# Moving the accumulating transfers of the mixer's weight sums from the attention to the v projection in a hybrid decoder block

## The chip, the cores and the metric

The kernel runs on one core of a Trainium2 chip. The metric is the device time of one execution in microseconds (us); the figure for a kernel is the median of its runs. An engine is named as in the profile: PE is TensorE (PEld its weight loads), DVE is VectorE, ACT is ScalarE, POOL is GpSimd, SP is SyncE, which here only issues transfers. `SPq` and `POOLq` are the instructions of those engines that issue or wait.

## The reference

One decoder block on 1024 tokens of width 1024, all in float32. Two branches read one normalised input: a state-space branch (`y_ssm`) and an attention with a forget gate. They are gated, added and multiplied by `w_mix_out`; then come a cross-attention, a gated feed-forward block and a last norm.

```python
u = rms_norm(h, norm_mix[l])
proj = u @ w_in[l]
u_ssm, q, k, v, f_logit, gate_logits = jnp.split(proj, [SPLIT_Q, SPLIT_K, SPLIT_V, SPLIT_F, SPLIT_G], axis=-1)
...
out_a = glu_a * jax.nn.sigmoid(glu_b)
att = forgetting_attention(q, k, v, f_logit + b_forget[l])
out_b = att @ w_fox_o[l]
gate_a, gate_b = jnp.split(jax.nn.sigmoid(gate_logits), 2, axis=-1)
h = h + (gate_a * out_a + gate_b * out_b) @ w_mix_out[l]
h = h + memory_cross_attention(...)
f_a, f_b = jnp.split(rms_norm(h, norm_ffn[l]) @ w_ffn_in[l], 2, axis=-1)
h = h + (jax.nn.silu(f_a) * f_b) @ w_ffn_out[l]
```

The forgetting attention has 8 heads of 64 and adds to each score the difference of running sums of `log_sigmoid(f_logit)`.

## The kernel before, in words

Every float32 operand is split into a high and a low part (`split`, lines 181 to 185: a cast on ACT into the high part, a subtraction on DVE or POOL into the low part), and a product is three matmuls (`mm3`, lines 172 to 175).

The program is written in stages: the input with its norms, the state-space stage with the gate products (its last instructions write `y_d` and `gate_d`), then `Fox.run`, and the tail from the mixer to the end. In `Fox.run` come, in the text, `prepare_v` (weights of v), eight `values_of_v` (the second half of v and the forget logits), `log_forget` (logarithms of the forget gates on DVE; it needs the small load `bfb`, line 1724), `setup` (constants on POOL, lines 1774 to 1784), four copies of `w_glu` in HBM into another order (`wg_d`, line 1990, 1 MB each), the projections of q and k for the first heads, `cumulate` (running sums, written to HBM as `cum_d`, lines 1762 and 1767), `gate_rows` (reads `cum_d` back into the rows 64 to 67 of the q and k tiles, lines 1840 and 1841), `row_max` for the first head (matmuls of line 1862, which read those rows), and then the loop over the 8 heads.

In that loop each head has 12 units (`scores`): scores on PE (lines 1892, 1893), the exponential on ACT (`pf`, line 1899), and the split of the result into `ph` and `pl`. For 4 of the 12 units the low part `pl` is made on POOL (line 1902), for the others on DVE. PE then multiplies `ph` (lines 1917, 1918) and `pl` (line 1924) with v. Between the units PE also gets the row maxima of the next head and the projection of the head after that.

A scheduler arranges the instructions of each engine ahead of time by its own estimates, keeping data dependences; so the place of an instruction on its engine is not that of its line in the text. `B.behind(ins)` only keeps what is issued in it behind `ins` where both are on the same engine. On the chip each engine then runs its list in order, and a transfer that must wait holds everything behind it on the engine that issues it.

The change is about `mix_sums` (lines 583 to 603). The mixer's product is computed with 7 instead of 8 block products, for which sums of blocks of `w_mix_out` are needed. They are made in HBM (`mt_d`), without any engine's arithmetic: a plain 1 MB copy issued by SP (`put`, line 590) writes one block, and two accumulating transfers of 512 KB issued by POOL (`add`, line 594) add another to it. The six steps depend on each other:

```python
steps = [lambda: (put(5, blk[0, 0]), put(7, blk[0, 1])), lambda: (add(5, 0, 1), add(7, 1, 1)),
         lambda: put(6, dst[5]), lambda: add(6, 1, 1), lambda: put(4, dst[6]), lambda: add(4, 1, 0)]
```

`put(6)` copies what `add(5)` finished, `add(6)` adds to that, `put(4)` copies its result, `add(4)` adds to it: on SP two of the four copies wait for POOL's transfers, and on POOL four of the eight wait for SP's copies. In the kernel before, step h - 1 is issued in the loop of head h, behind `self.spread[h - 1]` (a transfer of SP, line 1939), for h from 1 to 6. The results are read from line 754 on, in the tail.

Of the kernel before, what the change touches and what calls it, by code (L numbers as in the profile page):

```python
# [14 lines left out]
ALU = mybir.AluOpType  # L15
# [4 lines left out]
P = 128  # L20
# [4 lines left out]
NH = 8  # L25
# [9 lines left out]
NEG = -1.0e30  # L35
# [31 lines left out]
def f32(ap):  # L67
    return ap.bitcast(F32)
# [26 lines left out]
def weave(main, side, lead=0):  # L95

    n, m, done = len(main) - lead, len(side), 0
    for i, f in enumerate(main):
        f()
        want = m if i + 1 == len(main) else max(0, (i + 1 - lead) * m // max(n, 1))  # L100
        while done < want:
            side[done]()
            done += 1
# [1573 lines left out]
class Fox:  # L1677
# [69 lines left out]
    def cumulate(self):  # L1747

        B, fp, xl = self.B, self.fp, self.logf
        V, A, G, T, S = B.V, B.A, B.G, B.T, B.S  # L1750
        cum = fp.tile([NH, L], F32, tag="num", name="cum")
        ones8 = self.sh.half("ones8")[0:NH]
        G.memset(ones8, 1.0)
        for b in range(2):
            ps = B.bank(("misc", "pv")[b])
            for t in range(4):
                T.transpose(ps[0:NH, t * P:(t + 1) * P], xl[:, (4 * b + t) * NH:(4 * b + t + 1) * NH], B.ident)
            V.tensor_tensor_scan(out=cum[:, 512 * b:512 * b + 512], data0=ones8, data1=ps[0:NH, :],
                                 initial=0.0 if b == 0 else cum[:, 511:512], op0=ALU.mult, op1=ALU.add)
        cch = fp.tile([NH, L], F32R, tag="rb", bufs=2, name="cch")  # L1760
        A.copy(cch, cum)
        S.dma_start(self.cum_d[:, 0, :], f32(cch))
        for b in range(2):
            cs = slice(512 * b, 512 * b + 512)
            cl = fp.tile([NH, 512], F32R, tag="pl", bufs=4, name="cl")
            V.tensor_sub(cl, cum[:, cs], f32(cch[:, cs]))
            S.dma_start(self.cum_d[:, 1, cs], f32(cl))

    def setup(self):
        fp, G = self.fp, self.B.G  # L1770
        self.hb = [[self.sh.tmp("hb", F32R) if i == 0 else fp.tile([P, L], F32R, name=f"hb{s}") for s in range(4)]
                   for i in range(2)]
        for K1, K2, Q1, Q2 in self.hb:
            G.memset(f32(K1[64:69, :]), 1.0)
            G.memset(f32(Q1[64:69, :]), -1.0)

        self.tri = fp.tile([P, 512], F32, name="tri")
        G.memset(self.tri, 0.0)
        G.affine_select(out=self.tri[:, 384:512], in_=self.tri[:, 384:512], pattern=[[-1, P]], compare_op=ALU.is_ge,
                        fill=NEG, base=0, channel_multiplier=1)  # L1780
        self.trk = fp.tile([P, P], F32, name="trk")
        G.memset(self.trk, 0.0)
        G.affine_select(out=self.trk, in_=self.trk, pattern=[[1, P]], compare_op=ALU.is_ge, fill=NEG, base=0,
                        channel_multiplier=-1)
        self.maxed = self.scored = None
        self.pj, self.mc, self.pvs, self.num, self.rb, self.raw = {}, {}, {}, {}, {}, {}
        self.hi_todo, self.lo_todo, self.spread, self.maxima = [], [], {}, {}
# [170 lines left out]
    def run(self, y_d, yT, aT, w_glu, w_d, filler, sums):  # L1958
        B, fp, S = self.B, self.fp, self.B.S
        self.aT = aT  # L1960
        self.prepare_v()
        for t in range(NT):
            self.values_of_v(1, t)
        self.log_forget()
        self.setup()

        def load_y(k, h):

            with B.behind(self.maxima[NH - 2] if h else self.spread[NH - 4]):
                for i, dst in enumerate(yT.rhs(k, h)):  # L1970
                    S.dma_start(f32(dst).rearrange("p (t c) -> p t c", t=4),
                                y_d[k, i, 4 * h:4 * h + 4].rearrange("t p c -> p t c"))

        def first_glu(i, f):
            with B.behind(self.spread[3] if i < 9 else self.maxima[NH - 2]):
                f()

        def load_att(k):
            for h in range(2):
                for i, dst in enumerate(aT.rhs(k, h)):  # L1980
                    S.dma_start(f32(dst), self.att_d[i, k * P:(k + 1) * P, 512 * h:512 * h + 512])

        pro = [self.project(h) for h in range(NH)]
        for h in range(2):
            loaded = pro[h].load()
            pro[h].split()

        with B.tc.issue_after(loaded.ins):
            for k in range(4):
                S.dma_start(w_d[k].rearrange("(m g) c -> m g c", g=8),  # L1990
                            w_glu[k * P:(k + 1) * P].rearrange("(g m) c -> m g c", m=16))
        for f in pro[0].parts[:8] + pro[0].evac[:1] + pro[0].parts[8:] + pro[0].evac[1:]:
            f()
        self.values_of_v(0, 0)
        self.cumulate()
        for t in range(1, 4):
            self.values_of_v(0, t)
        for h in range(2):
            self.gate_rows(h)
        for f in pro[1].parts[:4]:  # L2000
            f()
        weave(pro[1].parts[4:8] + pro[1].evac[:1] + pro[1].parts[8:], self.row_max(0))
        pro[2].load()
        turned = self.max_row(0)
        with B.behind(self.negated):
            ready = pro[1].evac[1](pro[2].split)
        self.values_of_v(0, 4)
        pro[3].load()
        self.values_of_v(0, 5, ready)
        with B.behind(turned):  # L2010
            self.values_of_v(0, 6, ready)
        units = [(qc, kt) for qc in range(2) for kt in range(4 * qc + 4)]
        for h in range(NH):
            side = {i: [] for i in range(12)}
            late = h == NH - 2
            if late:
                for i, f in enumerate(pro[h + 1].parts[8:]):
                    side[i // 2].append(f)
                side[3].append(pro[h + 1].evac[1])
            if h + 1 < NH:  # L2020
                for i, f in enumerate(self.row_max(h + 1)):
                    side[(RSLOT_LATE if late else RSLOT)[i]].append(f)
                side[9].append(lambda: self.max_row(h + 1))
            if h + 2 < NH:
                n = 8 if h + 3 == NH else 16
                for i, f in enumerate(pro[h + 2].parts[:n]):
                    side[i if n == 8 else PSLOT[i]].append(f)
                side[9].append(pro[h + 2].evac[0])
                if n == 16:
                    side[11].append(pro[h + 2].evac[1])  # L2030
            if h + 3 < NH:
                side[9].append(lambda: pro[h + 3].split(self.exp))
            for n_ in {1: (4, 5), 2: (6,), 3: (7,)}.get(h, ()):
                side[5].append(lambda n_=n_: pro[n_].load(self.spread[h - 1]))
            if h == 0:
                side[0].append(lambda: self.values_of_v(0, 7))
            elif h < 7:
                side[5].append(lambda: sums[h - 1](self.spread[h - 1]))
            if late:
                for k in range(8):  # L2040
                    side[4 + k].append(lambda k=k: load_y(k % 4, k // 4))
            if h == NH - 1:
                for k in range(3):
                    side[6 + k].append(lambda k=k: load_att(k))
                for i, f in enumerate(filler):
                    side[i * 12 // len(filler)].append(lambda i=i, f=f: first_glu(i, f))
            for i, u in enumerate(units):
                self.scores(h, *u)
                for f in side[i]:
                    f()  # L2050
                if len(self.hi_todo) > 2:
                    self.values_hi()
                if len(self.lo_todo) > 1:
                    self.values_lo()
                if h and i == 5:
                    with B.behind(self.left):
                        self.divide(h - 1)
        while self.hi_todo:
            self.values_hi()
        while self.lo_todo:  # L2060
            self.values_lo()
        self.divide(NH - 1)
# [29 lines left out]
```

## Time and profile before

| | |
|---|---|
| median of 3 runs | 1574.99 us (1570.75 to 1575.76) |
| profiled execution | 1571.02 us |
| its span, first to last instruction | 1569.0 us |
| mean granted PE clock | 0.986 |
| busy: PE, DVE, ACT, POOL | 97%, 66%, 43%, 17% of the span |

The profile is of one execution. Its own time stands 2 us above its span and 4 us below the median of the runs. A timeline row gives the start in us from the span's start, the duration in us, the engine, the line, the operation, the tiles written and read, and in brackets the idle time of the engine before it and what ended that time. A row of the waits gives the total in us, the number of waits and the longest. A row of the windows gives a stretch, then for PE, PEld, DVE, ACT and POOL the busy us and the number of instructions, then the granted PE clock (1.00 is full), the mean busy share of the 16 DMA engines, and the GB/s that they moved. In the page, PEclk is the clock in tenths over 40 equal slices of 39.2 us.

### The profile page before, as it was taken

The page shows a single profiled execution, that of the slowest core. Times are in us where ns is not written, and L with a number is a line of the kernel's source. Part 1 is how long each engine was busy: PE and PEld are TensorE (multiplying, and loading weights), DVE is VectorE, ACT ScalarE, POOL GpSimd, SP SyncE. Part 2 cuts the span into 40 slices and gives each one's busy share as a digit, 9 for nine tenths or more (in the row PEclk, how much of TensorE's full clock was granted, in tenths as well). Part 3 has the DMA queues.
Part 4 walks back from the last instruction along what each step waited for, and adds up shares of the span by engine and source line. Part 5 has one row for each costly group of instructions (what it writes and reads, how often), then busy time and mean ns, then how long its engine had stood idle before and what let it go on. Part 6 is the DMA issues. An engine that isn't in the chain of part 4 may idle for free.

```text
span 1569.0 us, 20397 instructions
## 1 busy us (share of the span) xinstructions
PE 1521.0 (97%) x7281; PEld 1255.0 (80%) x7281; DVE 1039.4 (66%) x1860; ACT 668.2 (43%) x1187; POOL 268.6 (17%) x349
## 2 busy tenths in 40 slices
PE   8999999999967989999999999999999999999998
PEld 7888888998745768888888888888888888888886
DVE  7936454346645966969965687766677776575555
ACT  6423433325634744223645564333333333354343
POOL 1166641101121213320001200000000000101001
PEclk9999999999978999999999999999999999999999
DMA  9635556620544575856701156555544543797652
GB/s 284 157 104 102 129 136 131 193 24 8 116 75 88 133 205 144 273 174 235 241 29 53 55 212 196 164 162 162 163 155 156 160 147 128 275 393 234 198 161 107
DMA packets 201061, 245.59 MB, mean 157 GB/s; under 512 B 35736, under 2 KB 127816, under 8 KB 200448
## 3 DMA queue, kind: packets, MB, share of 16 engines
q1 hardware_dynamic: 191296, 222.27, 47.6%
q10 hardware_dynamic: 7488, 17.83, 3.0%
q0 software_dynamic: 2176, 4.19, 1.7%
q8 instruction: 57, 0.93, 0.2%
q14 instruction: 44, 0.36, 0.1%
HBM read 173.47 MB, written 81.10 MB: 162 GB/s over the span
## 4 chain that ended last, share of the span: by engine, by line
PE 87%; DVE 4%; DMA 3%; issue 2%; ACT 2%; POOL 1%; SPq 0%; POOLq 0%; DVEq 0%; ACTq 0%
PE mm L1064 15%; PE pv L1064 8%; PE mm L174 7%; PE mm L173 7%; PE mm L175 7%; PE mm L1207 5%; PE sc L1064 4%; PE sc L1207 4%; PE sc L173 3%; PE sc L175 3%; PE sc L174 3%; PE pv L1207 3%; PE mm L772 2%; DMA mt_d<-mt_d 2%; PE misc L1207 2%
## 5 line engine op out<-in xcount | busy, mean ns | idle before, releaser
L184 DVE TENSOR_TENSOR wlo<-raw,whi 128x1024 fp32r<-128x1024 f32 (+2 forms) x122 | 131.3, 1082 | 38.0 <-ACT whi L183 36.9
L183 ACT CAST whi<-raw 128x1024 fp32r<-128x1024 f32 (+2 forms) x122 | 110.8, 912 | 105.8 <-PE mm L174 38.2
L184 DVE TENSOR_TENSOR ol<-or,oh 128x1024 fp32r<-128x1024 f32 x73 | 90.3, 1240 | 73.8 <-ACT oh L183 72.8
L173 PE MATMUL mm<-uh,whi 128*128 128x512 f32 x344 | 138.0, 401 | 0.0
L174 PE MATMUL mm<-ul,whi 128*128 128x512 f32 x344 | 136.5, 397 | 0.0
L175 PE MATMUL mm<-uh,wlo 128*128 128x512 f32 x344 | 135.9, 395 | 0.0
L183 ACT CAST oh<-or 128x1024 fp32r<-128x1024 f32 x73 | 76.8, 1054 | 104.6 <-PE mm L1207 34.2
L1097 POOL TENSOR_TENSOR g<-a,c 128x512 f32<-128x512 f32 x22 | 35.7, 1622 | 389.3 <-ACT a L1096 389.3
L175 PEld LDWEIGHTS mm<-uh,wlo 128*128 128x128 f32 x344 | 65.6, 191 | 13.7 <-DVE wlo L184 0.2
L1899 ACT ACTIVATE pf<-sc 128x512 f32<-128x512 f32 (+1 forms) x96 | 46.5, 489 | 69.2 <-DVE sc L1895 36.6
L1902 POOL TENSOR_TENSOR pl<-pf,ph 128x512 fp32r<-128x512 f32 (+1 forms) x32 | 40.0, 1251 | 207.5 <-DVE ph L1901 201.7
L173 PEld LDWEIGHTS mm<-uh,whi 128*128 128x128 f32 x344 | 65.8, 191 | 11.9
L174 PEld LDWEIGHTS mm<-ul,whi 128*128 128x128 f32 x344 | 65.9, 192 | 11.3
L211 POOL TENSOR_TENSOR r<-ms,mhalf 128x1 f32<-128x1 f32 (+1 forms) x26 | 16.6, 645 | 294.2 <-DVE ms L207 252.8
L1086 DVE SCALAR_TENSOR_TENSOR c<-c,pv 128x512 f32<-128x512 f32 x22 | 15.1, 687 | 77.5 <-ACT c L1085 77.4
L1924 PE MATMUL pv<-pl,vhi 128*65 128x512 f32 (+1 forms) x96 | 33.8, 356 | 29.7 <-POOL pl L1902 29.3
L1064 PE MATMUL pv<-S3h,we 128*128 128x512 f32 x176 | 57.8, 389 | 0.0
L1905 DVE TENSOR_TENSOR pl<-pf,ph 128x512 fp32r<-128x512 f32 (+2 forms) x64 | 35.8, 564 | 20.4 <-ACT ph L1904 19.6
L1924 PEld LDWEIGHTS pv<-pl,vhi 128*65 128x65 f32 x96 | 13.5, 142 | 35.6 <-POOL pl L1902 30.6
L1351 POOL TENSOR_TENSOR sg<-sg,ga 128x512 f32<-128x512 f32 x16 | 29.3, 1852 | 74.0 <-DMA ga<-gate_d 38.6
L1207 PE MATMUL mm<-ol,oh 128*128 128x512 f32 (+1 forms) x110 | 41.9, 381 | 0.0
L1207 PE MATMUL mm<-oh,ol 128*128 128x512 f32 (+1 forms) x110 | 41.9, 381 | 0.0
(661 smaller groups left out, 4635.2 us busy)
## 6 DMA issues: line engine op xcount, KB each, us to landing
or<-c_d SPq DMA_DIRECT2D x77, 256.0 KB
wo<-in_w_ffn_out_dram SPq DMA_DIRECT2D x22, 512.0 KB
c_d<-g SPq DMA_DIRECT2D x44, 256.0 KB
t_d<-wo SPq DMA_DIRECT2D x44, 256.0 KB
or<-t_d SPq DMA_DIRECT2D x44, 256.0 KB
rawb<-in_w_ffn_in_dram SPq DMA_DIRECT2D x20, 512.0 KB
raw<-in_w_ffn_in_dram SPq DMA_DIRECT2D x20, 512.0 KB
raw<-in_w_in_dram SPq DMA_DIRECT2D x19, 512.0 KB
```

The costliest lines, as they stand in the source:

```text
L173: T.matmul(ps, lh, rh, start=first, stop=False)
L174: T.matmul(ps, lh, rl, start=False, stop=False)
L175: return T.matmul(ps, ll, rh, start=False, stop=last)
L183: cast = self.A.copy(hi, src)
L184: self.rest = (self.G if pool_lo else self.V).tensor_sub(lo, src, f32(hi))
L1064: T.matmul(ps, l_[:, k, :], r_, start=first and k == 0 and i == 0, stop=k == 3 and i == 2, skip_group_check=True)
L1097: G.tensor_mul(g[:, 512:], a1, c1)
L1207: T.matmul(ps, l_[:, gi], r_[:, c0:c1], start=k == 0 and (p == NP - LAST if own else p == 0 and n in (1, 2, 7)), stop=p == NP - 1 and k == ...
L1899: self.exp = A.activation(pf[:, off:], ps[:, off:], AF.Exp)
L1902: G.tensor_sub(pl[:, off:], pf[:, off:], f32(ph[:, off:]))
L1905: self.left = V.tensor_sub(pl[:, off:], pf[:, off:], f32(ph[:, off:]))
L1924: self.B.T.matmul(ps[0:65, off:], self.vh[kt // 2][:, kt % 2, h, :], pl[:, off:], start=False, stop=last)
```

## The change

`setup` is called ahead of the eight `values_of_v`, and right behind it all six steps of the sums, with `B.behind` on the last instruction of `setup` (the selection that finishes `trk`, on POOL). They are no longer issued in the loop over the heads. The constant `ones8` moves from `cumulate` into `setup`.

```diff
-        ones8 = self.sh.half("ones8")[0:NH]
-        G.memset(ones8, 1.0)
+        ones8 = self.ones8
...
+        self.ones8 = self.sh.half("ones8")[0:NH]
+        G.memset(self.ones8, 1.0)
         self.tri = fp.tile([P, 512], F32, name="tri")
...
-        G.affine_select(out=self.trk, in_=self.trk, pattern=[[1, P]], compare_op=ALU.is_ge, fill=NEG, base=0,
-                        channel_multiplier=-1)
+        self.ready = G.affine_select(out=self.trk, in_=self.trk, pattern=[[1, P]], compare_op=ALU.is_ge, fill=NEG,
+                                     base=0, channel_multiplier=-1)
...
         self.prepare_v()
+        self.setup()
+        for f in sums:
+            f(self.ready)
         for t in range(NT):
             self.values_of_v(1, t)
         self.log_forget()
-        self.setup()
...
-            elif h < 7:
-                side[5].append(lambda: sums[h - 1](self.spread[h - 1]))
```

On POOL, this is what stands before, from the last constant into the attention's fourth head (`pl` rows are the low parts, four to a head; `mt_d` rows are the accumulating transfers):

```order
L1783 AFFINE_SELECT trk<-trk 128x128
L1753 MEMSET ones_3398 8x512
L1902 TENSOR_TENSOR pl<-pf,ph 128x256
L1902 TENSOR_TENSOR pl<-pf,ph 128x512 x3
L1902 TENSOR_TENSOR pl<-pf,ph 128x256
L1902 TENSOR_TENSOR pl<-pf,ph 128x512 x3
L594 DMA mt_d<-in_w_mix_out_dram 128x2x512 x4
L1902 TENSOR_TENSOR pl<-pf,ph 128x256
L1902 TENSOR_TENSOR pl<-pf,ph 128x512 x3
L1902 TENSOR_TENSOR pl<-pf,ph 128x256
L1902 TENSOR_TENSOR pl<-pf,ph 128x512 x2
L594 DMA mt_d<-in_w_mix_out_dram 128x2x512
```

And this is POOL in the changed kernel, from the same constant:

```order
L1784 AFFINE_SELECT trk<-trk 128x128
L594 DMA mt_d<-in_w_mix_out_dram 128x2x512 x8
L1903 TENSOR_TENSOR pl<-pf,ph 128x256
L1903 TENSOR_TENSOR pl<-pf,ph 128x512 x3
L1903 TENSOR_TENSOR pl<-pf,ph 128x256
```

All eight transfers now stand in one row between the constants and the first `pl` of the first head.

On SP, this is what stands before, from the last stores of the state-space branch (`y_d`) to the read of the running sums:

```order
L1671 DMA y_d<-yh 128x1024
L1671 DMA y_d<-yl 128x1024
L1990 DMA wg_d<-in_w_glu_dram 128x1x2048
L1724 DMA bfb<-in_b_forget_dram 128x8
L1990 DMA wg_d<-in_w_glu_dram 128x1x2048 x3
L1762 DMA cum_d<-cch 8x1024
L1767 DMA cum_d<-cl 8x512 x2
L1800 DMA raw<-in_w_in_dram 128x8x64
L1801 DMA raw<-in_w_in_dram 128x8x64
L1840 DMA hb<-cum_d 2x1024
```

And in the changed kernel (the two rows `mt_d<-mt_d` are `put(6)` and `put(4)`):

```order
L1671 DMA y_d<-yh 128x1024
L1671 DMA y_d<-yl 128x1024
L1993 DMA wg_d<-in_w_glu_dram 128x1x2048
L590 DMA mt_d<-mt_d 128x4x512
L1724 DMA bfb<-in_b_forget_dram 128x8
L1993 DMA wg_d<-in_w_glu_dram 128x1x2048
L590 DMA mt_d<-mt_d 128x4x512
L1993 DMA wg_d<-in_w_glu_dram 128x1x2048 x2
L1761 DMA cum_d<-cch 8x1024
L1766 DMA cum_d<-cl 8x512 x2
L1801 DMA raw<-in_w_in_dram 128x8x64
L1802 DMA raw<-in_w_in_dram 128x8x64
```

Both dependent copies now stand ahead of the running sums, one of them ahead of `bfb` too; the other two copies, `put(5)` and `put(7)`, stand much earlier, here in the changed kernel among the first loads of the gate weights:

```order
L504 DMA kv_d<-kv 128x1024 x2
L158 DMA raw<-in_w_in_dram 128x4x256 x3
L590 DMA mt_d<-in_w_mix_out_dram 128x4x512
L158 DMA raw<-in_w_in_dram 128x4x256
L590 DMA mt_d<-in_w_mix_out_dram 128x4x512
L516 DMA u_d<-us 128x1024
```

They wait for nothing of the v projection, since `B.behind` on a POOL instruction holds only what POOL issues. PE's list is the same up to the attention, and inside the attention it differs by a few exchanges of neighbours.

## The prediction

> **What bounds the kernel now.** I read the page first, then PE's waits in the attention, then POOL's timeline there. PE is busy 97% of the span, so only places where PE stands still or runs slowly can give anything. The clock row of the page has one hole:
>
> ```profile
> span 1569.0 us, 20397 instructions
> PEclk9999999999978999999999999999999999999999
> ```
>
> The two low slices, the 12th and 13th, are those from 431 to 510 us, inside the attention. PE's waits from 397 to 586 us have one large row, and PE's timeline shows its three events:
>
> ```profile
> PE pv L1924 <- POOL pl L1902: 29.3, 3, 14.4
> 450.01 0.47 PE L1924 MATMUL pv<-pl,vhi 128*65 128x256 f32 x1 [14.37 <-POOL pl L1902]
> 500.19 0.69 PE L1924 MATMUL pv<-pl,vhi 128*65 128x512 f32 x1 [10.14 <-POOL pl L1902]
> 553.50 0.69 PE L1924 MATMUL pv<-pl,vhi 128*65 128x512 f32 x1 [4.80 <-POOL pl L1902]
> ```
>
> Each time PE needs a low part that POOL has not made. POOL's timeline says why:
>
> ```profile
> 424.44 1.36 POOL L594 DMA_DIRECT2D mt_d<-in_w_mix_out_dram  x1 [7.91 <-DMA mt_d<-in_w_mix_out_dram]
> 431.36 1.19 POOL L594 DMA_DIRECT2D mt_d<-in_w_mix_out_dram  x1 [5.57 <-issue]
> 438.10 1.15 POOL L594 DMA_DIRECT2D mt_d<-in_w_mix_out_dram  x1 [5.55 <-DMA rb<-rd_d]
> 448.05 1.16 POOL L594 DMA_DIRECT2D mt_d<-in_w_mix_out_dram  x1 [8.80 <-issue]
> 497.68 1.16 POOL L594 DMA_DIRECT2D mt_d<-in_w_mix_out_dram  x1 [15.91 <-DMA mt_d<-mt_d]
> 498.44 1.70 POOL L1902 TENSOR_TENSOR pl<-pf,ph 128x512 fp32r<-128x512 f32 x1
> 503.72 1.17 POOL L594 DMA_DIRECT2D mt_d<-in_w_mix_out_dram  x1 [3.59 <-issue]
> 543.22 1.16 POOL L594 DMA_DIRECT2D mt_d<-in_w_mix_out_dram  x1 [0.41 <-DMA mt_d<-mt_d]
> 551.00 1.15 POOL L594 DMA_DIRECT2D mt_d<-in_w_mix_out_dram  x1 [6.62 <-issue]
> DMA to landing us min/median/max: 5.7/6.6/9.6
> ```
>
> POOL does nothing else at those times: it waits for SP's copy, and between two accumulating transfers it stands as long as the first one takes to land (6.92, 6.74, 9.95, 6.04 and 7.78 us from one to the next, against landings of 5.7 to 9.6). The low part behind them is late by that much.
>
> **What is removed.** To price it with all that follows a stall, I cut the attention at each head's first exponential (line 1899), from head 1 (first row) to head 6 (second row), and took the windows between:
>
> ```profile
> 397.82 0.60 ACT L1899 ACTIVATE pf<-sc 128x512 f32<-128x512 f32 x1
> 560.14 0.60 ACT L1899 ACTIVATE pf<-sc 128x512 f32<-128x512 f32 x1 [5.75 <-DVE sc L1895]
> 397.82:427.60 29.78, 28.73 (x138) 21.53 (x136) 20.27 (x50) 17.84 (x34) 6.93 (x5) 1.00 0.58 136
> 427.60:469.28 41.68, 26.46 (x108) 20.06 (x109) 20.31 (x51) 16.09 (x32) 8.11 (x7) 0.71 0.50 82
> 469.28:506.93 37.65, 27.51 (x124) 20.58 (x123) 20.14 (x51) 16.74 (x33) 6.95 (x6) 0.86 0.43 80
> 506.93:532.81 25.88, 25.83 (x127) 19.20 (x126) 23.48 (x54) 19.71 (x37) 4.59 (x4) 1.00 0.47 110
> 532.81:560.14 27.33, 22.08 (x96) 16.16 (x96) 18.00 (x51) 13.02 (x27) 6.92 (x6) 0.88 0.85 211
> 560.14:585.02 24.88, 23.39 (x111) 16.49 (x111) 20.46 (x46) 14.67 (x28) 4.60 (x4) 1.00 0.67 178
> 420.62 5.83 DMA hb<-mr
> ```
>
> Head 4 (from 506.93) has no accumulating transfer on POOL: 25.88 us, with PE busy 25.83 of it at full clock. That is the price of a head with nothing in its way, and PE is then the bound, DVE (23.48) close behind. Heads 2 and 3 have the same work and take 15.8 and 11.8 us more. Head 1 takes 3.9 us more: the chain of waits has a 4 KB transfer of the row maxima (`hb<-mr`, last row) that took 5.83 us, issued right behind the two 1 MB copies of the sums. Head 5 has half the projection work of head 4, like head 6, which takes 24.88; so its clean time is between 25.88 x 96/127 = 19.6 (by the count of matmuls) and 24.9, the gain 2.4 to 7.7, and I take 5.0, near PE's own wait of 4.80. The sum is 3.9 + 15.8 + 11.8 + 5.0 = 36.5 us. Its bounds are 29.3 (the stalls alone, if the slow clock and the late maxima came from something else) and 39.2 (7.7 for head 5). Nothing else in the attention waits for the sums, and the tail reads them only after it.
>
> **What is moved, on POOL.** The chain of eight now starts when the constants are done and must end by the first `pl`:
>
> ```profile
> 292.17 0.29 POOL L1783 TENSOR_SCALAR_AFFINE_SELECT trk<-trk 128x128 f32<-128x128 f32 x1
> 375.22 0.74 POOL L1902 TENSOR_TENSOR pl<-pf,ph 128x256 fp32r<-128x256 f32 x1 [82.30 <-DVE ph L1901]
> ```
>
> POOL is idle for these 82 us, which covers the chain: eight intervals of 6.92 are 55 us, and the two copies on which it waits took 20.65 and 6.92 us in the attention, the first behind other loads:
>
> ```profile
> 476.63 20.65 DMA mt_d<-mt_d
> 535.89 6.92 DMA mt_d<-mt_d
> ```
>
> With 6.92 for all of them: `add(5)` starts at 292.5 and 299.4 and lands at 306.0; `add(7)` starts at 306.3 and 313.2; `put(6)` leaves SP at 306.1 and lands at 313.0, so `add(6)` follows without a gap at 320.1 and 327.0 and lands at 333.6; `put(4)` leaves at 333.7 and lands at 340.6; `add(4)` ends near 355. That is 20 us before the first `pl`, so POOL costs nothing; without this cover each us late is a us for the first head.
>
> **What is moved, on SP.** Here is the cost. SP's transfers before, the read of the forget bias on DVE, PE's first row maximum with the pass of its wait, and two windows of the DMA engines:
>
> ```profile
> 291.83 0.78 SPq L1990 DMA_DIRECT2D wg_d<-in_w_glu_dram  x1
> 292.71 1.12 SPq L1724 DMA_DIRECT2D bfb<-in_b_forget_dram  x1
> 293.88 7.09 SPq L1990 DMA_DIRECT2D wg_d<-in_w_glu_dram  x3
> 339.76 0.30 SPq L1762 DMA_DIRECT2D cum_d<-cch  x1
> 342.65 0.26 SPq L1840 DMA_DIRECT2D hb<-cum_d  x1
> 323.97 0.22 DVE L1728 TENSOR_TENSOR logf<-fl,bfb 128x64 f32<-128x64 f32 x1
> 351.73 0.22 PE L1862 MATMUL pv<-hb 68*128 68x128 f32 x1
> L1862 PEldq EVENT_SEMAPHORE x1: 51/51/51, 349.6 to 349.6; - x1
> 292.00:309.00 17.00, 17.00 (x119) 15.95 (x118) 3.85 (x8) 4.31 (x7) 0.92 (x3) 1.00 0.95 328
> 343.00:350.00 7.00, 7.00 (x44) 6.28 (x44) 0.42 (x1) 0.37 (x1) 0.00 (x0) 1.00 0.86 98
> ```
>
> `put(6)` now holds SP from 292.7 to 306.1; `bfb` stands behind it and lands with it near 314, 10 us before DVE reads it: hidden. `put(4)` holds SP until 333.7, and two `wg_d` copies stand behind it. In the window from 292 us such copies ran at 328 GB/s, so 1.05 MB takes 3.2 us. If transfers of one queue come out in order, the queue is empty at 340.6 + 6.4 = 347.0. `cum_d`, ready at 339.8 as before, lands near 348, where before `hb<-cum_d` could be issued at 342.65 because it had landed: 5.4 us later. The projection loads (0.5 MB, at 98 GB/s 5.3 us) stand between, as before. PE's wait was passed at 349.6 and its matmul ran at 351.73, so 2.1 us are to spare. PE stands for 5.4 - 2.1 = 3.3 us at its first row maximum; its list goes on in order, so everything after is later by as much. PE also runs slowly behind a stall: head 5, with one of 4.80 us, has a mean clock of 0.88, so 0.12 x 27.33 = 3.3 us of full-clock work is gone, a part of it in the stall itself; I add 2.5 us: 5.8. With the mean interval of 7.49 instead of 6.92 the chain is 3.4 us longer and the cost 9. I take 7. The bounds: 0 with the shortest interval (6.04: `put(4)` 5 us earlier, all covered), and 16 if three of the five intervals ahead of `put(4)` take 9.95, as one beside other traffic did.
>
> The Trainium skill's page "DMA: Bandwidth & Descriptors" (Queues, rings and completion order) says that a DMA engine takes turns between the queues that have work for it, packet by packet; `add(7)` runs beside `put(6)` and a `wg_d` copy, so by that rule it is among the slow ones, and the cost goes towards 16 and the time to 1554.5. In the trace the interval of 9.95 us against 6.04 speaks for the rule, but the window of each is too mixed to show it.
>
> `put(5)` and `put(7)` go among the first loads of gate weights. At 328 GB/s they take 6.4 us; the only load between them is a gate weight too, and the last split of those on ACT waited for PE and not for its load:
>
> ```profile
> 91.52 1.05 ACT L183 CAST whi<-raw 128x1024 fp32r<-128x1024 f32 x1 [3.86 <-PE mm L174]
> ```
>
> So they are free; were they not covered they would cost at most their 6.4 us. `ones8` is a 0.5 us memset on an idle POOL, either way.
>
> The sum is -36.5 + 7 = -29.5 us. The profiled execution took 1571.0 us (span 1569.0), so it would become 1541.5. The runs shown have a median of 1575.0, 4 above it, and I carry the difference over: 1545.5 us.
>
> **The rivals.**
>
> *The accumulating transfers are quick and the copies hide altogether.* With all intervals at 6.04 or below, `put(4)` leaves before 329 and `cum_d` finds an empty queue. The cost is 0 and the time 1575 - 36.5 = 1538.5. For it: SP issued nothing from 301 to 339.8 us before, so there is room, and 5.7 us is the shortest landing. Against it: only one of five intervals was that short, and wg_d copies come in between. The same page of the Trainium skill (Anatomy of one DMA) fits 2.0 us plus bytes over 436e3, an estimate of 3.2 us for 512 KB, and by it this rival would be the answer; the trace's 5.7 to 9.6 for these transfers disagree and decide.
>
> *Slower: SP's head of line becomes the bound.* If the intervals are 9.95, `add(5)` lands at 312; if `put(6)` takes 20.65 it lands at 333, and `add(6)` then at 353; `put(4)` with 20.65 more lands at 374, the two `wg_d` copies at 381, `hb` near 390. PE then stands 38 us at the first row maximum and 2.5 more at a slow clock: 40.5 against 36.5, so 1579. It decides when `put(4)` leaves later than about 360. For it: SP runs in order, and both prices are in the trace. Against it: the 20.65 us copy stood behind projection loads that are not there now.
>
> *The stalls go but not all that I put down to them.* Only the 29.3 us of PE's own waits come back, because the slow clock and the late maxima have other causes (`hb<-mr` still stands behind the projection loads, PE's order has changed a little): 1575 - 29.3 + 7 = 1552.7. For it: DVE is at 23.48 of 25.88 us in the clean head. Against it: that clean head is in the trace.
>
> That the change doesn't do what it says is ruled out by the order of POOL's list, where no transfer stands among the `pl` any more.
>
> **How the numbers follow.** Forecast 0.55, quick transfers 0.17, smaller gain 0.16, SP as the bound 0.12. A measurement of this kernel can tell about 0.3%, 4.7 us, from no change. All of the first three are faster by more: 0.88. Of the last, costs of 32 to 41 us are within 0.3% (0.05), and beyond that slower (0.07). The low end takes the larger gain at no cost, 1575 - 39.2 = 1535.8, less the 4 us by which runs differ: 1532. The high end takes the smaller gain and the larger cost, 1575 - 29.3 + 16 = 1561.7, so 1562. What is left out is nearly only the rival of SP.
>
> **What would show it.** Right: PE has no wait for POOL in the attention, heads 2 and 3 take about 26 us, the page's clock row loses its hole there, and PE has one wait of 2 to 6 us at line 1862 (1863 in the changed text) near 352 us. The chain on POOL ends before 365. Wrong: a wait of over 15 us at that line, DVE waiting for `bfb` before 330 us, a first `pl` that waits for a transfer, or heads 2 and 3 still above 30 us.

## The result, and the profile after

The changed kernel takes 1549.8 us (median of 4 runs, 1547.5 to 1551.9), beside 1572.9 for the kernel before in the same session (1570.3 to 1575.8). The ratio is 0.985 with a 95% interval of 0.983 to 0.988: faster by 23 us where 29.5 were predicted, at 1545.5. The time lies in the range of 1532 to 1562. Gain and cost both came out larger than forecast, the cost by more.

The page after, its span and clock row, and PE's waits from 280 to 640 us:

```profile
span 1548.6 us, 20398 instructions
PEclk9999999997999999999999999999999999999999
PE pv L1863 <- DMA hb<-cum_d: 17.3, 1, 17.3
PE mm L1863 <- DVE mc L1868: 1.2, 1, 1.2
```

The hole of two slices in the attention is gone, and so are the 29.3 us of waiting for POOL's low parts. In their place stands one wait of 17.3 us, for the read of the running sums, where the forecast had a stall of 3.3. It makes the new hole in the clock row, the tenth slice. PE's timeline has it at the first row maximum:

```profile
369.55 0.44 PE L1863 MATMUL pv<-hb 68*128 68x128 f32 x1 [17.30 <-DMA hb<-cum_d]
```

The attention after, cut again at each head's first exponential, heads 1 to 6:

```profile
417.31:444.75 27.44, 25.70 (x127) 19.64 (x126) 21.32 (x50) 17.27 (x32) 4.59 (x4) 1.00 0.34 69
444.75:469.52 24.77, 24.74 (x123) 18.83 (x123) 20.24 (x51) 16.74 (x32) 4.61 (x4) 1.00 0.32 55
469.52:494.32 24.80, 24.76 (x123) 18.86 (x123) 20.28 (x51) 16.75 (x33) 4.61 (x4) 1.00 0.31 55
494.32:520.31 25.99, 25.69 (x127) 19.33 (x127) 23.53 (x54) 19.75 (x37) 4.61 (x4) 1.00 0.37 93
520.31:540.33 20.02, 19.31 (x95) 13.89 (x95) 18.08 (x51) 13.03 (x26) 4.59 (x4) 1.00 0.73 182
540.33:564.76 24.43, 23.72 (x114) 17.04 (x113) 19.71 (x46) 15.14 (x29) 4.61 (x4) 1.00 0.77 195
```

Against the same rows of before, head 1 gained 2.3 us, head 2 16.9, head 3 12.9, head 5 7.3, head 6 0.5, and head 4 lost 0.1: 39.8 us in all. But head 1 begins at 417.31 instead of 397.82, 19.5 us later. The two make 20.3 us, and the spans differ by 20.4 (1569.0 - 1548.6); nothing is left for any other place.

Where the 19.5 us come from is read on POOL and SP. Of the eight accumulating transfers on POOL the first two and the last three, with the first low part behind them, and the shortest, middle and longest time from the issue of the eight to their landing:

```profile
293.34 1.36 POOL L594 DMA_DIRECT2D mt_d<-in_w_mix_out_dram  x1
307.74 1.19 POOL L594 DMA_DIRECT2D mt_d<-in_w_mix_out_dram  x1 [13.04 <-issue]
...
341.17 1.15 POOL L594 DMA_DIRECT2D mt_d<-in_w_mix_out_dram  x1 [4.78 <-issue]
354.71 1.15 POOL L594 DMA_DIRECT2D mt_d<-in_w_mix_out_dram  x1 [12.38 <-DMA mt_d<-mt_d]
368.50 1.15 POOL L594 DMA_DIRECT2D mt_d<-in_w_mix_out_dram  x1 [12.64 <-DMA raw<-in_w_in_dram]
394.71 0.74 POOL L1903 TENSOR_TENSOR pl<-pf,ph 128x256 fp32r<-128x256 f32 x1 [25.06 <-DVE ph L1902]
DMA to landing us min/median/max: 5.6/10.2/14.1
```

SP at the same time, from `put(6)` to the read of the running sums:

```profile
316.12 0.59 SPq L590 DMA_DIRECT2D mt_d<-mt_d  x1
...
347.92 0.55 SPq L590 DMA_DIRECT2D mt_d<-mt_d  x1
348.51 1.28 SPq L1993 DMA_DIRECT2D wg_d<-in_w_glu_dram  x2
349.88 0.47 SPq L1761 DMA_DIRECT2D cum_d<-cch  x1
...
360.53 0.25 SPq L1841 DMA_DIRECT2D hb<-cum_d  x1
```

`put(4)` leaves at 347.92 instead of the forecast 333.7, because the six accumulating transfers ahead of it (`add(5)`, `add(7)`, `add(6)`) took 54.6 us (293.34 to 347.92) instead of 41. `cum_d`, ready near 339.8 as before, is held on SP until 349.88, and then goes out behind three copies; `hb<-cum_d` is issued at 360.53 where it was 342.65. Two reasons add up: 10.1 us for which SP was held, and 7.8 more between the two issues (10.65 against 2.89). The first row maximum starts 17.8 us later for it (369.55 against 351.73). The rest up to 19.5 goes with a slow clock behind the stall: 0.81 from 369.55 to 380.00, where the same work had 1.00 before.

### The profile page after: what moved, and what is told of

The parts are those of the page before. It is cut to its first block, busy times and chain, and to the rows that moved or that the text cites. A ratio compares the mean times of both kernels' runs of the same rounds, so it can differ in the third digit from the quotient of the medians.

```text
span 1548.6 us, 20398 instructions
## 1 busy us (share of the span) xinstructions
PE 1511.8 (98%) x7281; PEld 1249.5 (81%) x7281; DVE 1039.5 (67%) x1860; ACT 668.2 (43%) x1187; POOL 266.9 (17%) x349
## 4 chain that ended last, share of the span: by engine, by line
PE 84%; DVE 5%; issue 4%; DMA 3%; ACT 2%; POOL 1%; SPq 0%; POOLq 0%; DVEq 0%; ACTq 0%
PE mm L1064 15%; PE pv L1064 8%; PE mm L173 7%; PE mm L174 7%; PE mm L175 7%; PE mm L1207 5%; PE sc L1064 4%; PE sc L1207 4%; PE pv L1207 3%; PE sc L173 3%; PE sc L175 3%; PE sc L174 3%; PE misc L1207 2%; PE mm L772 1%; PE sc L772 1%
## 5 line engine op out<-in xcount | busy, mean ns | idle before, releaser
L175 PEld LDWEIGHTS mm<-uh,wlo 128*128 128x128 f32 x344 | 65.0, 189 | 13.4 <-DVE wlo L184 0.2
L1903 POOL TENSOR_TENSOR pl<-pf,ph 128x512 fp32r<-128x512 f32 (+1 forms) x32 | 36.9, 1152 | 175.4 <-DVE ph L1902 136.5
L1207 PE MATMUL mm<-oh 128*128 128x512 f32 (+1 forms) x110 | 41.9, 381 | 0.0
L1085 ACT COPY c<-mm 128x512 f32<-128x512 f32 x22 | 12.9, 587 | 65.2 <-PE mm L1064 65.2
```

The lines of the kernel that those rows point to most:

```text
L175: return T.matmul(ps, ll, rh, start=False, stop=last)
L1207: T.matmul(ps, l_[:, gi], r_[:, c0:c1], start=k == 0 and (p == NP - LAST if own else p == 0 and n in (1, 2, 7)), stop=p == NP - 1 and k == ...
L1903: G.tensor_sub(pl[:, off:], pf[:, off:], f32(ph[:, off:]))
```

## The experiments

Theory: the gain is POOL no longer standing in the attention; the cost is `put(4)`, which waits on SP in front of `cum_d` for a chain that traffic slows down. The rivals are that a part of the gain belongs to something else that moved, that the wait comes from the copies queued in front of `cum_d` whatever holds SP, and that the transfers are slow without any traffic.

**Where the gain comes from.** Three kernels. First a control, only the early constants:

```diff
 (changed kernel)
         self.setup()
-        for f in sums:
-            f(self.ready)
...
+            elif h < 7:
+                side[5].append(lambda: sums[h - 1](self.spread[h - 1]))
```

> A control: the changed kernel with the constants early (and ones8 among them) but all six steps of the sums back in the loop over the heads, as before. If the constants carry none of the effect, the time is that of the kernel before, 1571 within 4, with its stalls for POOL in the attention. Rival: the exchanges of neighbours on PE that come with the moved constants carry a part of the gain, and the time falls by 5 to 10 us.

Measured: 1571.0 us beside 1571.2, ratio 0.9997 (0.998 to 1.001), with the waits for POOL all there:

```profile
PE pv L1925 <- POOL pl L1903: 30.1, 3, 14.6
```

So the constants and the exchanges of neighbours that come with them carry nothing.

Then the accumulating transfers left out, once in each kernel:

```diff
 (kernel before; and in another kernel the same in the changed one)
         for p in (0, 2):
-            B.G.dma_start(dst[n][:, p:p + 2], blk[i, j, :, p:p + 2], accum_op=ALU.add)
+            pass
```

> The kernel before with the eight accumulating transfers left out (the sums in HBM lack those terms); the four copies of SP stay in the attention. Theory: the whole gain comes from POOL standing at its accumulating transfers, with the stalls of PE and the slow clock that follow them. Then the time falls by 36 to 40 us, to 1533 to 1537, heads 2 and 3 take 25 to 27 us, and the clock row has no hole. Rival: a part belongs to SP's copies (the late row maxima of head 1, 2 to 4 us, the weight loads behind 1 MB copies) or to the moved constants and PE's changed order: then heads 1 to 3 keep 3 to 11 us of it, and the time is 1537 to 1544.

Measured: 1541.4 us, ratio 0.981 (0.979 to 0.982). This is the rival's range: 30.0 us are gone, and not the 38 or so that both parts are worth. Heads 1, 3 and 4 are still not clean, and PE waits for the row maxima in head 3:

```profile
397.88:428.13 30.25, 28.49 (x138) 21.63 (x136) 21.22 (x50) 17.87 (x34) 4.60 (x4) 1.00 0.53 132
452.61:483.14 30.53, 26.03 (x122) 19.39 (x121) 20.38 (x51) 16.86 (x32) 4.61 (x4) 0.95 0.36 79
483.14:510.58 27.44, 27.17 (x127) 20.77 (x126) 23.59 (x54) 19.85 (x36) 4.61 (x4) 0.94 0.37 88
481.55 0.80 PE L1892 MATMUL sc<-hb 69*128 69x512 f32 x1 [4.50 <-DMA hb<-mr]
```

SP's list in that head shows what stood in front of them:

```profile
459.90 6.29 SPq L590 DMA_DIRECT2D mt_d<-mt_d  x1
466.29 5.00 SPq L1951 DMA_DIRECT2D att_d<-ahi  x1
...
474.47 0.72 SPq L1880 DMA_DIRECT2D hb<-mr  x1
```

`put(6)` here waits for nothing, and still the small transfer behind it lands so late that PE goes on 7 us after its issue (481.55 against 474.47). The head takes 5.7 us more than in the changed kernel (30.53 against 24.80), the next one 1.5 more, and head 1, with the two other copies, 2.8 more.

> The changed kernel with the eight accumulating transfers left out (the sums in HBM lack those terms); SP's four copies stay where the change put them and wait for nothing. The kernel before without the transfers kept 10.6 us of loss in the attention, by the starts of the heads, against the changed kernel; the theory is that SP's 1 MB copies make it there, with the row maxima of heads 1 and 4 queued behind them. Then the attention takes 176 us here, as in the changed kernel, cum_d goes out near 340, PE waits under 3 us at line 1863, and the time is 1531 to 1534, 8 to 10 us under the kernel before without the transfers (1541.4). Rival: those 10.6 us are of the order on PE and not of the copies; they are gone either way, but then put(6) and put(4) ahead of cum_d cost something of their own without the transfers: a wait of 5 us or more at line 1863 and 1537 or more.

Measured: 1532.9 us, ratio 0.975 (0.973 to 0.976), with no wait over 0.5 us in the attention and `cum_d` on time:

```profile
339.65 0.30 SPq L1761 DMA_DIRECT2D cum_d<-cch  x1
```

As the theory had it: SP's copies were worth 8.5 us where they stood (1541.4 - 1532.9), and PE waits for none of them at the new place as long as they need not wait themselves. That gives the balance of the change from medians: 30.0 for POOL's transfers and 8.5 for SP's copies, 38.4 against the kernel before (1571.4 - 1532.9, rounded), less the 16.9 that the chain costs now (1549.8 - 1532.9). It leaves 21.5 and not 23, because the medians are of several sessions, in which that of the kernel before was between 1571.2 and 1572.9.

**What the cost is.** The two last steps behind the reads of `cum_d` (`gate_rows` now returns its last read):

```diff
-        for f in sums:
+        for f in sums[:4]:
             f(self.ready)
...
         for h in range(2):
-            self.gate_rows(h)
+            rows = self.gate_rows(h)
+        sums[4](rows)
+        sums[5](self.ready)
```

> The changed kernel with only put(4) and add(4) issued behind the reads of cum_d instead of ahead of its writes; the other six accumulating transfers and put(5), put(6), put(7) stay where the change put them. Theory H (the hold): put(4) waits on SP until 347.9 us for add(6), cum_d behind it is issued at 349.9 instead of 339.8, and that makes the wait of 17.3 us at the first row maximum. Then cum_d goes out near 340 here, PE waits under 3 us at line 1863 and the time is 1549.8 - 17 to 1549.8 - 13: 1533 to 1537. The adds stay as slow as in the changed kernel (intervals of 6 to 14 us), which costs nothing. Rival Q (the queue): the wait is mostly the 8 to 9 us that a transfer takes behind others on SP's queue, whatever holds SP; the three wg_d copies still stand ahead of cum_d, so a wait of 7 to 10 us stays and the time is 1540 to 1543. A third outcome, put(4) in front of the projection's weight loads now delays those: a wait of 5 to 10 us of PE for raw loads in its place, 1540 to 1545.

Measured: 1543.8 us, ratio 0.982 (0.981 to 0.984), with runs from 1537.4 to 1547.8. In the trace (of the fastest) the wait at line 1863 is gone, although all `wg_d` copies still stand ahead of `cum_d`; PE waits for something else:

```profile
PE sc L1893 <- DMA hb<-mr: 2.4, 1, 2.4
340.34 0.30 SPq L1761 DMA_DIRECT2D cum_d<-cch  x1
348.17 0.57 SPq L590 DMA_DIRECT2D mt_d<-mt_d  x1
364.53 32.29 SPq L1881 DMA_DIRECT2D hb<-mr  x2
```

So holding SP was the cause of the wait (theory H): without the hold the `wg_d` copies have drained by 340. The median is not in that theory's range, though: the third outcome came with it, a late transfer behind `put(4)`; more on it below.

The `wg_d` copies moved instead, behind the first row maximum:

```diff
-        with B.tc.issue_after(loaded.ins):
-            for k in range(4):
-                S.dma_start(w_d[k].rearrange("(m g) c -> m g c", g=8),
-                            w_glu[k * P:(k + 1) * P].rearrange("(g m) c -> m g c", m=16))
...
         turned = self.max_row(0)
+        with B.behind(self.maxima[0]):
+            for k in range(4):
+                S.dma_start(w_d[k].rearrange("(m g) c -> m g c", g=8),
+                            w_glu[k * P:(k + 1) * P].rearrange("(g m) c -> m g c", m=16))
```

> The changed kernel with the four wg_d copies behind the first row maximum; put(4) still stands ahead of cum_d on SP. Theory C (traffic): an accumulating transfer lands in 6 to 7 us alone and in 10 to 14 beside transfers of SP's queue. With the 2.1 MB of wg_d gone from there the intervals on POOL fall to 6 to 8 us, except the first beside the stores of y_d and gate_d; put(4) leaves near 333 to 338, cum_d near 340 to 342, the wait at line 1863 is 0 to 3 us and the time is 1533 to 1538. Rival G (the transfers are slow by themselves when POOL issues them here, or from something other than wg_d): intervals stay near 9.6 us on average, put(4) leaves near 348 as before; only the two wg_d copies behind it are gone, the wait is 10 to 14 us and the time 1543 to 1547.

Measured: 1536.9 us, ratio 0.978 (0.976 to 0.979). The time is in theory C's range, but not for C's reason. The scheduler drew two projection loads into the gap, and the second interval became the longest of all; SP was held until 347.00, and PE waited 5.4 us:

```profile
303.32:319.24 15.92, 15.92 (x134) 15.92 (x133) 2.83 (x12) 2.24 (x6) 1.20 (x2) 1.00 0.62 88
347.00 0.48 SPq L1761 DMA_DIRECT2D cum_d<-cch  x1
PE pv L1863 <- DMA hb<-cum_d: 5.4, 1, 5.4
```

It tells the two parts of the wait apart: with SP held 7 us but nothing of `wg_d` in front of `cum_d`, 5.4 us of PE are lost; with a hold of 10 and two `wg_d` copies behind it, 17.3.

Both edits together:

> Both edits together: put(4) with add(4) behind the reads of cum_d, and the four wg_d copies behind the first row maximum. Under either theory of the slow intervals nothing but put(6) is left on SP ahead of cum_d, so PE's wait at line 1863 is under 2 us and the time is 1533 to 1536, the gain in the attention (39.8 us by the starts of the heads) without the cost. If the wg_d copies beside the attention's loads cost what they cost ahead of it, or put(4) delays the projection's loads, it is slower than the kernel with put(4) alone moved, by 2 to 6 us.

Measured: 1532.5 us, ratio 0.975 (0.974 to 0.976), runs from 1531.0 to 1533.1, and no wait for a transfer in the attention. That is the time of the kernel without the accumulating transfers (1532.9), so nothing of their cost is left.

**Why the intervals are long.** The quiet kernel, with the `wg_d` copies and the projection loads of heads 2 and 3 behind the first row maximum (the diff above, and in addition):

```diff
-        pro[2].load()
         turned = self.max_row(0)
...
+        pro[2].load(self.maxima[0])
...
-        pro[3].load()
+        pro[3].load(self.maxima[0])
```

> The changed kernel with the four wg_d copies and the projection weight loads of heads 2 and 3 both behind the first row maximum, so that between the stores of y_d and put(4) SP moves only bfb and put(6). In the kernel with the wg_d copies alone moved, the projection loads had moved up in their place and the second interval was 15.9 us. Theory C (traffic makes the intervals long): the first interval, beside the stores, is 8 to 12 us, all others ahead of put(4) are 5.8 to 7; add(5) lands near 309, put(6) lands near 317, put(4) leaves before 333, cum_d goes out near 340, no wait at line 1863. The time is 1531 to 1535 if the late loads cost nothing in the first head, 2 to 6 more if they do. Rival G (long by themselves): the intervals still have a mean of 9 or more and put(4) leaves after 343.

The windows from each accumulating transfer to the next, first in the changed kernel (five), then in the quiet one (the first four; the sum is of six, with the window from the last transfer to `put(4)`). The last two columns are the busy share of the DMA engines and their GB/s:

```profile
293.34:307.74 14.40, 14.40 (x101) 13.50 (x101) 3.38 (x7) 4.12 (x7) 1.36 (x1) 1.00 0.78 223
307.74:316.32 8.58, 8.58 (x74) 8.58 (x73) 1.46 (x6) 1.04 (x3) 1.19 (x1) 1.00 0.41 63
316.32:328.77 12.45, 12.45 (x77) 11.06 (x76) 7.70 (x28) 3.51 (x7) 1.15 (x2) 1.00 0.74 213
328.77:335.25 6.48, 6.48 (x40) 5.78 (x39) 5.26 (x17) 2.82 (x5) 1.16 (x1) 1.00 0.58 81
335.25:341.17 5.92, 5.92 (x53) 5.74 (x52) 4.16 (x6) 2.85 (x5) 1.15 (x1) 1.00 0.56 89
```

```profile
293.26:303.98 10.72, 10.72 (x70) 9.82 (x70) 2.87 (x3) 3.37 (x5) 1.36 (x2) 1.00 0.70 195
303.98:310.05 6.07, 6.07 (x52) 6.07 (x51) 1.07 (x5) 0.74 (x2) 1.19 (x1) 1.00 0.56 89
310.05:318.44 8.39, 8.39 (x72) 8.39 (x71) 1.49 (x6) 1.12 (x3) 1.15 (x2) 1.00 0.73 188
318.44:324.75 6.31, 6.31 (x42) 5.62 (x41) 3.71 (x9) 2.74 (x4) 1.16 (x1) 1.00 0.58 83
sum 44.09, PE 44.09 PEld 40.92 DVE 19.71 ACT 13.04 POOL 7.15; mean PE 7.35 PEld 6.82 DVE 3.29 ACT 2.17 POOL 1.19
```

Alone, an interval is 5.9 to 6.5 us, and the DMA engines move 80 to 90 GB/s. Beside the stores of `y_d` and `gate_d` it is 10.7, with a `wg_d` copy as well 14.4; beside `put(6)` it is 8.4, with a `wg_d` copy as well 12.5. The six transfers take 44.1 us instead of 54.6, `cum_d` goes out on time at 340.04, and PE does not wait for `hb<-cum_d`. So traffic makes the long intervals. One does not fit: the 8.58 us from 307.74, in which nearly nothing but the transfer itself moved (0.52 of 0.54 MB); why it was slow is not shown. `put(4)` left at 337.4, later than the 333 expected; the interval beside `put(6)`, put at 7 us at most, is a part of that. The time missed: 1546.3 us, ratio 0.983 (0.982 to 0.985), 13.4 above the kernel without the transfers, where 2 to 6 had been allowed for the late loads. The time is lost in heads 0 and 1, with 71.9 us from 368.64 to 440.56 where the changed kernel has 56.1 (388.65 to 444.75); in the first stretch PE is busy for 18.87 of 23.22 us, at a clock of 0.78:

```profile
368.64:391.86 23.22, 18.87 (x72) 11.64 (x72) 7.61 (x19) 10.08 (x20) 4.57 (x4) 0.78 0.70 148
```

PE has 72 matmuls there, where the whole head 0 of the changed kernel has 151 (from 388.65 to 417.31). The late `wg_d` copies alone do not do this, since the kernel with both edits has them at the same place; whether the loads are late by their own place or by the copies in front of them, no run parts.

Then the same bytes in smaller pieces:

```diff
-        for p in (0, 2):
-            B.G.dma_start(dst[n][:, p:p + 2], blk[i, j, :, p:p + 2], accum_op=ALU.add)
+        for p in range(4):
+            B.G.dma_start(dst[n][:, p:p + 1], blk[i, j, :, p:p + 1], accum_op=ALU.add)
```

> The changed kernel with each accumulating transfer of 512 KB cut into two of 256 KB: sixteen instead of eight. Between two transfers POOL stands until the first has landed, though nothing in the program makes it. Theory R (room): POOL can hold only so much of a transfer under way, 512 KB fill it, and halves fit side by side: then some of the sixteen go out 1.2 us behind the one before, the landings overlap, and the five intervals ahead of put(4) shrink from 47.8 us to 25 to 35; put(4) leaves before 338, the wait is under 4 us, the time 1533 to 1538. Rival L (POOL waits for each landing, whatever its size, and a landing is mostly a fixed time): sixteen intervals of 4 us or more, put(4) leaves later than 347.9, the wait at line 1863 grows beyond 17.3 us and the time is 1555 or more. Rival B (a landing is bytes): two halves take as long as one whole, the time stays at 1549.8 within 4.

Measured: 1537.9 us, ratio 0.978 (0.977 to 0.980). POOL and SP in the traced execution, which is the fastest of five (1534.3), and PE's wait:

```profile
292.77 2.75 POOL L594 DMA_DIRECT2D mt_d<-in_w_mix_out_dram  x3
305.46 0.84 POOL L594 DMA_DIRECT2D mt_d<-in_w_mix_out_dram  x1 [9.95 <-issue]
...
321.82 2.50 POOL L594 DMA_DIRECT2D mt_d<-in_w_mix_out_dram  x3 [8.11 <-DMA mt_d<-mt_d]
```

```profile
332.15 0.55 SPq L590 DMA_DIRECT2D mt_d<-mt_d  x1
332.75 1.27 SPq L1993 DMA_DIRECT2D wg_d<-in_w_glu_dram  x2
339.57 0.30 SPq L1761 DMA_DIRECT2D cum_d<-cch  x1
PE pv L1863 <- DMA hb<-cum_d: 2.5, 1, 2.5
```

Three pieces of 256 KB go out in a row, and the fourth waits. Two of 512 KB never did. That fits theory R, that POOL has room for so much under way and stands when it is used up; if bytes count, the limit lies between 768 KB and 1 MB. `add(5)`, `add(7)` and `add(6)` take 39.4 us, close to the 41 of the prediction, and so this kernel also tries out the rest of the prediction's step: `put(4)` leaves at 332.15 (forecast 333.7) with the two `wg_d` copies behind it, and PE's stall is 2.5 us (forecast 3.3).

**What is left of the cost.** In the kernel with the two last steps behind the reads, 11 us to the best one were open. First `add(4)` left out of it:

```diff
         sums[4](rows)
-        sums[5](self.ready)
```

> The kernel with put(4) and add(4) behind the reads of cum_d (1543.8, with five runs from 1537.4 to 1547.8, the fastest of them profiled) without add(4): the last two accumulating transfers are left out, so one block of the sums lacks a term. It asks where that kernel lost 11 us against the one that also moved the wg_d copies (1532.5). Theory P: add(4) is issued at 355.8 and 370.9, each takes 14 to 15 us to land, and the first low part on POOL is due at 380, so in the slower runs it stands behind the second. Without it the spread goes and the time is 1533 to 1537. Rival S: put(4) stands on SP ahead of two projection loads and the first hb<-mr, which PE waited for by 2.4 us in the profiled run and for longer in the others. Then the time stays at 1540 to 1546 and PE still waits for hb<-mr.

Measured: 1536.5 us, ratio 0.977 (0.973 to 0.980), runs from 1531.6 to 1545.1. The median is P's, 7 us lower, but the spread stays, and so does S's wait, 3.0 us for `hb<-mr` in the profiled run: `add(4)` may have a share (the runs of the two kernels overlap), and is not the whole. Nor does the trace of the kernel with `add(4)` show POOL late: its last transfer is issued at 370.89, and the first low part, at 380.02, waits for `ph`. In the run without `add(4)`, `put(4)` left at 355.07, 7 us later than in the one shown above, with the projection loads and `hb<-mr` behind it. Then `put(4)` moved past them, nothing left out:

```diff
 (changed kernel)
-        for f in sums:
+        for f in sums[:4]:
             f(self.ready)
...
         turned = self.max_row(0)
+        sums[4](self.maxima[0])
+        sums[5](self.ready)
```

> The same with put(4) and add(4) kept but put(4) moved on by three rows of SP, behind the projection loads and the first hb<-mr; nothing is left out. Theory S (put(4) ahead of hb<-mr is the loss): PE no longer waits for hb<-mr, 1533 to 1537. Theory P (add(4) beside the first low parts): add(4) now starts near 372 and ends near 385, later than the first low part is due, so PE waits for POOL at the first head by 5 to 10 us, and the time is 1540 to 1547.

Measured: 1532.3 us, ratio 0.974 (0.971 to 0.976), runs from 1530.0 to 1533.5. PE waits for no transfer in the attention. POOL shows how close `add(4)` comes:

```profile
376.68 1.15 POOL L594 DMA_DIRECT2D mt_d<-in_w_mix_out_dram  x1 [4.93 <-issue]
377.40 1.19 POOL L1903 TENSOR_TENSOR pl<-pf,ph 128x256 fp32r<-128x256 f32 x1
```

The first low part stands right behind the last transfer, some 2 us later than it was due, and PE does not feel it. It starts 0.7 us after that transfer was issued, and so does not wait for its landing. So theory S holds for where `put(4)` stands, and P's fear of the first low part does not. Why leaving `add(4)` out of the other kernel gave 7 us stays open; only one execution of each is traced. With this edit alone the change is worth 40 us (1572.4 to 1532.3) instead of 23; it and the kernel with both edits are the best of all, and cannot be told apart.

## Why the prediction was right, and which step was too small

**By its own signs.** No wait for POOL in the attention, heads 2 and 3 near 26 us and no hole in the clock there: these came as written. The wait at line 1863 is 17.3 us and not 2 to 6, which is past the 15 us that the prediction itself named as a sign of being wrong, and POOL's chain did not end before 365. That the time is only 4.3 us from the forecast is in part luck. From one profiled execution to the other the change took 20.6 us (1571.0 to 1550.4) where 29.5 were forecast; but the 4 us by which the median of before stood above its profiled run were carried over, and after the change the median is 0.6 below it.

**The stalls in the attention.** Right in mechanism, and 39.8 us where 36.5 were forecast. Heads 2 and 3 were put at 25.9 us and take 24.8, since the clean head 4, by which they were priced, does more work (PE 25.69 busy against 24.75); head 5 gained 7.3 of the 2.4 to 7.7 allowed. One attribution was wrong: the 11.8 us of head 3 were put down to POOL alone. Without the transfers that head keeps 5.7 us, from `put(6)` in front of the row maxima, the mechanism that the prediction named only for head 1. It did no harm to the sum, because the change moves the copies too. The rival with the smaller gain had half of the truth: POOL's transfers alone are worth 30.0 us, near its 29.3, and SP's copies brought the rest.

**POOL's cover.** The chain was to end near 355; its last transfer was issued at 368.50 and lands after that, too late for "before 365". It cost nothing, and would have cost nothing without the stall: the first low part was due at 375.22, and a low part behind a transfer waits for its issue (over at 369.65), not for its landing, as the kernel with `put(4)` moved shows. So the cover was larger than the prediction had it.

**SP, the step that failed.** "With 6.92 for all of them": the middle interval of the attention (the mean is 7.49) was laid into a stretch with the stores of `y_d`, `wg_d` copies and `put(6)`. The six transfers ahead of `put(4)` took 54.6 us (9.1 each) instead of 41. Everything behind that number worked as written: `put(4)` left 14.2 us late, which on the forecast stall of 3.3 makes 17.5, and 17.3 were measured; with 39.4 us in place of 54.6 the wait is 2.5. The hold on SP and the copies piled up behind it were both in the forecast. Behind the stall come 2.2 us more (19.5 in all; for the slow clock 2.5 had been added). The upper bound of 16 was too low for the same reason: it let three intervals be slow, at 9.95, the slowest of the attention, and here two were above 12.

**The page's rule.** The Trainium skill's page "DMA: Bandwidth & Descriptors" (Queues, rings and completion order) has each DMA engine take turns between its queues, packet by packet, and the prediction noted that the cost would then go towards 16. The traces agree in direction: 5.9 to 6.5 us alone (but for the 8.58), 8.4 beside one copy, 12.5 and 14.4 with a second copy or store; the turns themselves no trace here shows. It should have moved the value taken, not only the range.

**The small terms.** `bfb`, the early `put(5)` and `put(7)` and the constants cost nothing, as said: PE waits for nothing from 60 to 340 us. The slower rival (SP at the head of the line, 40.5 us) had the right place, but less than half its price came; `put(6)` did not take 20.65 us, its bytes were through by 328.77, within 12.7 us of its issue.

## What to carry to other kernels

A transfer that depends on another queue's chain does not belong in front of a small load that PE needs soon: its wait holds the whole queue, and what piles up behind it costs again. Price a chain of transfers by the traffic at the place where it will stand, from a window there, not by the interval usual at the place that it leaves. And where large copies move together with the work they belong to, ask what they cost by themselves; here that was 8.5 us, in head 3 through a 4 KB transfer queued behind them.

## What the runs showed of the hardware

Accumulating transfers of 512 KB from HBM to HBM landed 5.5 us after issue at best, and with nothing beside them they follow each other at 5.8 to 6.5 us, but once at 7.2 and once at 8.58 (with `add(4)` left out, and in the changed kernel). POOL lets three of 256 KB run side by side but not two of 512 KB; what the limit counts is not shown. An interval of 15.9 us stood beside projection loads (rows of 64 elements) with only 88 GB/s on the engines, and the one of 8.58 had 63 GB/s; bytes alone do not explain these two. The first had 2737 packets (0.66 MB) of SP's queue beside it, where the 8.4 us beside `put(6)` in the quiet kernel had 528 (1.05 MB): more packets with fewer bytes took longer. No run here isolates either.
